# Down products of four feed-forward layers as seven block products

## The chip, the cores and the metric

One core of one Trainium2 chip runs the whole program in one launch. The metric is the device time of an execution in microseconds (us); lower is better. The median of the runs before is 3422.52 us.

## The reference, cut to what matters

Three network blocks are applied one after the other to x, 512 tokens of 1024 features, all in float32. Four feed-forward layers are in them; each has a wide first product, a nonlinearity, and a product back to 1024 features, the *down product*:

```
# layers 1 and 2 (first block): 2816 hidden features
x = layer_norm(ALPHA * x + 0.5 * ((silu(x @ w_gate) * (x @ w_up)) @ w_down))
# layer 3 (second block): 2816 hidden features, a short convolution over tokens on both halves
h = gelu(conv(u[..., :2816])) * conv(u[..., 2816:]);   x = x + rmsnorm(h @ w_down)
# layer 4 (third block): 4096 hidden features
x = x + gt2 * (square(relu(h @ w1)) @ w2)
```

Between the layers stand three mixers (attention, state-space and delta nets), which the change leaves as they are, but for where their temporaries lie.

## The kernel before, in words

Every float32 operand of the large products is held as two float32r tiles, high digits and low digits, so that a product is three matmuls: high x high, low x high, high x low. A matmul is 128 x 128 by 512 columns.

**Weights.** `slab` (L262 to L274) loads 1024 columns of weights into a `raw` tile (three buffers, DMA on the SP queue), makes the high digits `whi_t` by a cast on ACT (L268) and the low digits `wlo_t` by a subtraction on DVE (L272). `whi_t` and `wlo_t` have three buffers each, so the cast of a new slab waits until TensorE has read an old one for the last time. In some stages POOL takes a part of L272's columns.

**Feed-forward layers.** `ffn` (L630) cuts the hidden features into chunks of four tiles of 128 (the first chunk of layers 1 to 3 has two; these layers have six chunks, layer 4 has eight). Within a chunk, `hidden` runs `fm` (L338 to L340) for two tiles at a time: gate and then up weights in layers 1 to 3, the one matrix in layer 4. A call of `fm` is two slabs of 24 matmuls. The result is taken out of PSUM by ACT and DVE (L698 and L702 in layers 1 and 2, L1188 and L1191 in layer 3, L1527 and L1528 in layer 4) and split into digits (`split`, L257 on ACT and L258 on POOL or DVE). The down product of a chunk, `tm` (L379 to L381), follows the next chunk's first two hidden tiles (the first four in layer 4): four slabs, each used for all four tiles of 128 tokens, 24 matmuls a slab, 96 in all. Its sums are added on DVE to an SBUF tile (L709 in layers 1 and 2, L1214 in layer 3, L1537 in layer 4), eight times 128x512 a chunk. The last chunk goes through `tail` (L452 to L454).

**What sets the order.** Each engine runs its instructions in a fixed order, made when the program is built; a slab's cast and subtraction stand some places ahead of the matmuls that need them. In layer 2, `fill` also puts between the hidden tiles the third block's `modulation` (L1249 to L1262): 48 loads of 512 KB, each multiplied and added on DVE (L1249, L1251), and six times a split and two short products whose sums DVE adds to a row (L1262).

```
due = hh, hl, f1 - f0, f0          # a chunk's hidden features, for `tm` one step later
for c in range(2):
    self.linear_tm(down, due[2], range(c * 512, c * 512 + 512), due[:2], ..., k0=due[3])
```

Of the kernel before, what the change touches and what calls it, by code (L numbers as in the profile page):

```python
# [8 lines left out]
F32 = mybir.dt.float32  # L9
# [6 lines left out]
P = 128  # L16
# [6 lines left out]
SPACE = 25 * 1024 - 320  # L23
# [10 lines left out]
def constants():  # L34
    """What depends on shapes alone: masks and distances, each [P, n]."""
# [36 lines left out]
class Space:  # L72
    """Columns of a tile that parts of the computation take and give back."""

    def __init__(self, pool, n, dt, name):
        self.ap = pool.tile([P, n], dt, name=name)
        # when each granule was given back last, or None while it is taken
        self.free, self.clock = [0] * (n // GRAIN), 0

    def take(self, n):  # L80
        """The offset of n columns: those that have been free for longest."""
        g = -(-n // GRAIN)
        free, best, run = self.free, None, 0
        for i, f in enumerate(free):
            run = run + 1 if f is not None else 0
            if run >= g:
                edge = (i < g or free[i - g] is None) + (i + 1 == len(free) or free[i + 1] is None)
                key = (max(free[i - g + 1:i + 1]), -edge, i)
                if edge and (best is None or key < best):
                    best = key  # L90
        if best is None:
            raise MemoryError("no room for %d columns in %d" % (n, GRAIN * sum(f is not None for f in free)))
        a = best[2] - g + 1
        free[a:a + g] = [None] * g
        return a * GRAIN

    def give(self, a, n):
        self.clock += 1
        g = -(-n // GRAIN)
        self.free[a // GRAIN:a // GRAIN + g] = [self.clock] * g  # L100


class Room:
    """Tiles for a part of the computation, which leave() gives back; a tag names a ring of `bufs` of them."""

    def __init__(self, net, bufs=1):
        self.net, self.bufs, self.rings = net, bufs, {}

    def tile(self, shape, dt=F32, tag=None, name=None, bufs=None):
# [3 lines left out]
        if tag not in self.rings:  # L113
            self.rings[tag] = [0, n, space, [space.take(n) for _ in range(bufs or self.bufs)]]
# [4 lines left out]
        t = space.ap[:shape[0], a:a + n]  # L119
# [12 lines left out]
class Rows:  # L132
    """Tiles of four tiles of features each, read as one."""

    def __init__(self, tiles):
        self.tiles = tiles

    def __getitem__(self, at):
        return self.tiles[at[1] // 4][(at[0], at[1] % 4) + at[2:]]


class Net:
    def __init__(self, ctx, tc, shapes):
# [9 lines left out]
        self.spaces = {F32: Space(sp, SPACE, F32, "space"), F32R: Space(sp, SPACE_R, F32R, "space_r")}  # L153
        self.xt = pool("xt", 1)
        self.vec = Room(self, 3)
# [9 lines left out]
    def masks(self):  # L165
        """What all parts use; the first products come before."""
# [9 lines left out]
    def lay(self, shape, recipe):  # L176
        """An input of the program: `recipe` lays it out from the kernel's own."""
# [22 lines left out]
    def columns(self, pool, name, parts):  # L200
        """Vectors of features with features on partitions, a column for each 128: [P, sum of rows]."""
# [3 lines left out]
    def rowvec(self, name, n=D, off=0, pool=None, tag="vec"):  # L205
        """A vector of features on every partition."""
# [1933 lines left out]
```

## Time and profile before

| | |
|---|---|
| runs (us) | 3422.52, 3427.88, 3419.94; median 3422.52 |
| profiled execution, first to last instruction | 3421.3 us span |
| TensorE busy | 3302.2 us, 97% |
| VectorE (DVE) busy | 1910.4 us, 56% |
| ScalarE (ACT) busy | 1302.5 us, 38% |
| GpSimd (POOL) busy | 704.7 us, 21% |
| weight loads | 530 of 512 KB, 3.3 us from issue to landing (median) |

The profiled execution's own time is known by its span, which is 1.2 us under the median of the runs. A busy TensorE is one whose matmuls follow each other; their modelled ends overlap, so the distance of two starts tells the rate. Columns of a group of instructions: line, engine, operation, output and inputs, shapes, count, busy us, mean ns of one, idle time before them and who ended it.

### The profile page before, as it was taken

How to read it: one execution, taken by the hardware profiler on the slowest of the kernel's cores; microseconds unless marked ns; L12 is line 12 of the kernel's file. 1: busy time of each engine (PE TensorE's matmuls, PEld its weight loads, DVE VectorE, ACT ScalarE, POOL GpSimd, SP SyncE). 2: the span in 40 equal slices, each digit the busy share in tenths (PEclk: the TensorE clock that was granted, in tenths of full speed). 3: DMA queues.
4: the chain of work that ended last, by engine and by line, in shares of the span. 5: the costliest groups of instructions: out<-in, count | busy, mean ns of one | idle time of the engine just before them, and what ended most of it. 6: DMA issues, size and time to landing. Idle time of an engine off the chain costs nothing. (4 is left out here: it accounts for less than half of the span.)

```text
span 3421.3 us, 41640 instructions
## 1 busy us (share of the span) xinstructions
PE 3302.2 (97%) x16104; PEld 2687.0 (79%) x16104; DVE 1910.4 (56%) x2922; ACT 1302.5 (38%) x2158; POOL 704.7 (21%) x569
## 2 busy tenths in 40 slices
PE   9999999999999999988999999998999999999998
PEld 8888877777787888876777888887876777788886
DVE  4333657567648565565544465556676475463445
ACT  4222367233333322244342353333366222244333
POOL 0110301334323111132102240003210224130003
PEclk9999999999999999999999999999999999999999
DMA  5222321221225454331132332222411212232222
GB/s 196 95 99 98 136 70 56 77 77 65 83 87 195 155 174 166 130 137 65 64 105 87 111 113 99 99 93 99 137 56 50 71 53 78 93 118 105 99 97 88
DMA packets 105254, 348.59 MB, mean 102 GB/s; under 512 B 13836, under 2 KB 19020, under 8 KB 104800
## 3 DMA queue, kind: packets, MB, share of 16 engines
q1 hardware_dynamic: 105056, 345.93, 29.4%
q8 instruction: 127, 2.08, 0.2%
q14 instruction: 71, 0.58, 0.1%
HBM read 337.46 MB, written 8.42 MB: 101 GB/s over the span
## 5 line engine op out<-in xcount | busy, mean ns | idle before, releaser
L272 DVE TENSOR_TENSOR wlo_t<-raw,whi_t 128x1024 fp32r<-128x1024 f32 (+3 forms) x538 | 674.4, 1255 | 742.5 <-ACT whi_t L268 721.3
L268 ACT CAST whi_t<-raw 128x1024 fp32r<-128x1024 f32 (+1 forms) x538 | 560.6, 1043 | 1160.9 <-PE acc L339 614.7
L338 PE MATMUL acc<-xhi,whi_t 128*128 128x512 f32 x2160 | 856.9, 397 | 0.0
L339 PE MATMUL acc<-xlo,whi_t 128*128 128x512 f32 x2160 | 849.9, 393 | 0.0
L340 PE MATMUL acc<-xhi,wlo_t 128*128 128x512 f32 x2160 | 847.8, 393 | 0.0
L338 PEld LDWEIGHTS acc<-xhi,whi_t 128*128 128x128 f32 x2160 | 406.9, 188 | 88.2 <-issue 9.5
L339 PEld LDWEIGHTS acc<-xlo,whi_t 128*128 128x128 f32 x2160 | 407.2, 189 | 82.6 <-issue 4.8
L340 PEld LDWEIGHTS acc<-xhi,wlo_t 128*128 128x128 f32 x2160 | 406.9, 188 | 83.1 <-issue 0.7
L379 PE MATMUL acc<-whi_t,space_r 128*128 128x512 f32 x752 | 293.3, 390 | 1.2 <-DVE space L709 1.2
L380 PE MATMUL acc<-whi_t,space_r 128*128 128x512 f32 x752 | 293.1, 390 | 1.0 <-DVE space_r L258 1.0
L381 PE MATMUL acc<-wlo_t,space_r 128*128 128x512 f32 x752 | 292.3, 390 | 0.0
L258 POOL TENSOR_TENSOR space_r<-space,space_r 128x512 fp32r<-128x512 f32 x44 | 81.2, 1848 | 524.7 <-ACT space_r L257 524.7
L379 PEld LDWEIGHTS acc<-whi_t,space_r 128*128 128x128 f32 x752 | 141.2, 188 | 31.7 <-ACT whi_t L268 1.6
L380 PEld LDWEIGHTS acc<-whi_t,space_r 128*128 128x128 f32 x752 | 141.2, 188 | 30.9 <-DVE space_r L258 1.9
L381 PEld LDWEIGHTS acc<-wlo_t,space_r 128*128 128x128 f32 x752 | 141.2, 188 | 29.3
L338 PE MATMUL acc<-space_r,whi_t 128*128 128x512 f32 x384 | 152.0, 400 | 0.4 <-ACT space_r L257 0.4
L339 PE MATMUL acc<-space_r,whi_t 128*128 128x512 f32 x384 | 150.9, 393 | 0.0
L340 PE MATMUL acc<-space_r,wlo_t 128*128 128x512 f32 x384 | 150.7, 393 | 0.0
L379 PE MATMUL acc<-whi_t,xhi 128*128 128x512 f32 (+1 forms) x384 | 149.8, 390 | 0.4 <-ACT space L247 0.4
L257 ACT CAST space_r<-space 128x512 fp32r<-128x512 f32 x139 | 85.7, 618 | 158.9 <-DVE space L702 60.7
L381 PE MATMUL acc<-wlo_t,xhi 128*128 128x512 f32 (+1 forms) x384 | 143.7, 374 | 0.0
L380 PE MATMUL acc<-whi_t,xlo 128*128 128x512 f32 (+1 forms) x384 | 143.7, 374 | 0.0
(448 smaller groups left out, 5193.1 us busy)
## 6 DMA issues: line engine op xcount, KB each, us to landing
raw<-in SPq DMA_DIRECT2D x530, 512.0 KB, 3.3
space<-in SPq DMA_DIRECT2D x69, 512.0 KB, 4.4
space<-in SPq DMA_DIRECT2D x25, 256.0 KB, 3.7
x_keep<-space SPq DMA_DIRECT2D x12, 512.0 KB, 3.5
space<-x_keep SPq DMA_DIRECT2D x12, 512.0 KB, 4.4
space<-mod SPq DMA_DIRECT2D x6, 512.0 KB
space<-in SPq DMA_DIRECT2D x2, 1024.0 KB
raw<-in SPq DMA_DIRECT2D x8, 256.0 KB, 2.6
```

The lines of the kernel that those rows point to most:

```text
L257: self.nc.scalar.copy(dhi, src)
L258: (eng or self.nc.vector).tensor_sub(dlo, src, dhi.bitcast(F32))
L268: nc.scalar.copy(hi[:, :n], raw[:, :n])
L272: eng.tensor_sub(lo[:, c], raw[:, c], hi[:, c].bitcast(F32))
L338: nc.tensor.matmul(ps[j], whi[:, k, f], xhi[:, kk], start=kk == 0, stop=False)
L339: nc.tensor.matmul(ps[j], whi[:, k, f], xlo[:, kk], start=False, stop=False)
L340: nc.tensor.matmul(ps[j], wlo[:, k, f], xhi[:, kk], start=False, stop=kk == K - 1)
L379: nc.tensor.matmul(ps, xhi[:, kk, t], whi[:, k], start=kk == 0, stop=False)
L380: nc.tensor.matmul(ps, xlo[:, kk, t], whi[:, k], start=False, stop=False)
L381: nc.tensor.matmul(ps, xhi[:, kk, t], wlo[:, k], start=False, stop=kk == K - 1)
```

## The change

The down product of every chunk but a layer's last is done by seven block products in place of eight. Tokens, hidden features and output columns are halved each: a block is 256 tokens by half of the chunk's hidden tiles by 512 output columns. Seven sums and differences of hidden blocks (the *sides*) and seven of weight blocks are multiplied, and the products accumulate in two pairs of PSUM tiles, from which DVE adds or subtracts the running sums into the result.

- `sides` makes for each pair of hidden tiles, from four blocks of 256 tokens in a tile `t8`, four further blocks (L666 on POOL, L667 and L668 on DVE) and the digits of seven (three casts L670 on ACT, three subtractions L671 on POOL, of 256, 1024 and 512 columns).
- `seven` loads the four weight blocks into tiles `wd` of their own (L684) and adds them up in place (L695, on DVE; in layer 3 on POOL), four times a chunk; each of seven steps splits its block (L275 on ACT, L276 on DVE; buffers of `whi_t` and `wlo_t` as before), does 12 matmuls (L706) into the PSUM pairs `sc`, `sc` or `tr`, `o`, and hands both to `done` (L837, or L1276 in layers 3 and 4).
- `paced` puts the steps one by one between the 12-matmul pieces of the next chunk's `fm`.
- `modulation` takes its PSUM from `acc` in place of `sc`; 3584 columns of SBUF change hands between float32 temporaries and float32r operands (`lend`); the residual of layers 1 and 2 is scaled in place; small temporaries are placed by another rule. The digits of the last chunk's hidden features are made on POOL in all layers.

```diff
+    A12, A22, Z5, S3, S2, S4, A11, A21 = range(8)
+    def sides(self, t8, hi, lo, eng):
+        nc = self.nc
+        both = slice(self.Z5, self.S3 + 1)
+        eng.tensor_sub(t8[:, both], t8[:, self.A22:self.A11 + 1:5], t8[:, self.A21][:, None, :].to_broadcast([P, 2, 256]))
+        nc.vector.scalar_tensor_tensor(t8[:, self.S2], t8[:, self.S3], -1.0, t8[:, self.A22], op0=ALU.mult, op1=ALU.subtract)
+        nc.vector.scalar_tensor_tensor(t8[:, self.S4], t8[:, self.S2], -1.0, t8[:, self.A12], op0=ALU.mult, op1=ALU.subtract)
+        for g in (slice(self.A11, self.A11 + 1), slice(self.Z5, self.A11), slice(0, self.Z5)):
+            nc.scalar.copy(hi[:, g], t8[:, g])
+            eng.tensor_sub(lo[:, g], t8[:, g], hi[:, g].bitcast(F32))
+    def seven(self, wp, w, k0, sides, done, eng):
...
+        for i in (0, 1, 3, 2):
+            raw[i] = wp.tile([P, WS], F32, tag="wd", name="wd", bufs=4)[:, :n * 512]
+            nc.sync.dma_start(raw[i], src[i])
+        b11, b12, b21, b22 = (raw[i] for i in range(4))
+        steps = ((self.A11, b11, None, 0, True, (0, 0), 1), (self.Z5, b11, b12, 1, True, (1, 1), -1),
+                 (self.S2, b11, b22, 0, False, (0, 1), -1), (self.S4, b22, None, 1, False, (0, 1), -1),
+                 (self.S3, b12, b22, 0, False, (1, 1), -1), (self.A12, b21, None, 1, True, (0, 0), 1),
+                 (self.A22, b11, b21, 0, False, (1, 0), 1))
...
+        for slot, b, more, bank, start, c, sign in steps:
+            if more is not None:
+                eng.tensor_add(b, b, more)
...
+            self.split(hi[:, :n * 512], lo[:, :n * 512], b)
...
+            if start:
+                ps[bank] = [self.psum(x) for x in (("sc", "sc"), ("tr", "o"))[bank]]
+            for r in range(2):
+                t = slice(r * P, r * P + P)
+                for k, (ah, al) in enumerate(sides):
+                    for i, (x, y) in enumerate(((ah, whi), (al, whi), (ah, wlo))):
+                        nc.tensor.matmul(ps[bank][r], x[:, slot, t], y[:, k], start=start and k + i == 0,
+                                         stop=k == n - 1 and i == 2, skip_group_check=not start)
+                tt = 2 * c[0] + r
+                done(tt, c[1], (tt, c[1]) not in seen, sign, ps[bank][r])
+                seen.add((tt, c[1]))
+            yield
...
             for w, K, cols, ev in reversed(parts):
-                self.linear_fm(w, K, cols, X, ev)
+                for _ in self.fm(w, K, cols, X, ev):
+                    self.due_next()
...
-                    if due:
-                        for c in range(2):
-                            self.linear_tm(down, due[2], range(c * 512, c * 512 + 512), due[:2],
-                                           lambda tt, ps, c=c: done(tt, c, due[3] == 0, ps), k0=due[3])
-                        due = None
-                due = hh, hl, f1 - f0, f0
+                while self.due:
+                    self.due_next()
+                if not plain:
+                    at, both = f0, [sides[i] for i in range((f1 - f0) // 2)]
+                    self.due = self.paced(self.seven(tp, down, at, both, lambda tt, c, f, sign, ps, at=at: done(tt, c, f and at == 0, sign, ps),
+                                                     eng or nc.vector), lead, 14 if step == 2 else 7, prep)
...
+    def paced(self, parts, lead, n, prep):
+        for _ in range(lead):
+            yield
...
+        for i in range(1, n - lead + 1):
+            while done * (n - lead) < 7 * i:
+                next(parts)
+                done += 1
+            yield
...
-            self.ffn(X, DFF // P, 2, hidden, "ffn_w_down_2", done, part, end)
+            self.ffn(X, DFF // P, 2, hidden, "ffn_w_down_2", done, part, end, eng=nc.gpsimd)
...
-                    ps = self.psum("sc")
+                    ps = self.psum()
```

The order of the instructions moves with it. DVE in layer 1, one chunk's turn before: the slabs' low digits (L272), the sums out of PSUM (L709) in fours, and the hidden tiles (L702):

```order
L272 TENSOR_TENSOR wlo_t_647<-raw_645,whi_t_646 128x1024
L709 SCALAR_TENSOR_TENSOR space_70<-acc_575,space_70 128x512
L709 SCALAR_TENSOR_TENSOR space_70<-acc_576,space_70 128x512
L709 SCALAR_TENSOR_TENSOR space_70<-acc_577,space_70 128x512
L709 SCALAR_TENSOR_TENSOR space_70<-acc_578,space_70 128x512
L272 TENSOR_TENSOR wlo_t_681<-raw_679,whi_t_680 128x1024
L272 TENSOR_TENSOR wlo_t_711<-raw_709,whi_t_710 128x1024
```

The same place now (L290 is `slab`'s subtraction, L276 that of a step, L695 the adding of weight blocks, L837 the sums out of PSUM, L830 a hidden tile):

```order
L276 TENSOR_TENSOR wlo_t_1289<-space_70,whi_t_1288 128x1024
L695 TENSOR_TENSOR space_70<-space_70 128x1024 x2
L276 TENSOR_TENSOR wlo_t_1322<-space_70,whi_t_1321 128x1024
L695 TENSOR_TENSOR space_70<-space_70 128x1024
L837 SCALAR_TENSOR_TENSOR space_70<-sc_1292,space_70 128x512
L837 SCALAR_TENSOR_TENSOR space_70<-sc_1293,space_70 128x512
L290 TENSOR_TENSOR wlo_t_1343<-raw_1341,whi_t_1342 128x1024
L276 TENSOR_TENSOR wlo_t_1362<-space_70,whi_t_1361 128x1024
L837 SCALAR_TENSOR_TENSOR space_70<-tr_1325,space_70 128x512
L695 TENSOR_TENSOR space_70<-space_70 128x1024
```

The sums out of PSUM come in twos, and between them stand the weight blocks' sums and the low digits of steps and slabs.

ACT in layer 4, between the first and the third step of a chunk, now (L1662 and L1664 are the relu and the square of a hidden tile, L670 the sides' high digits, L275 a step's cast, 23771 the second step and 23792 the third, 23822 the fourth):

```order
L670 CAST flex_22379<-space_70 128x256
L275 CAST whi_t_23771<-space_70 128x1024
L1662 ACTIVATE space_70<-acc_23652 128x512
L1664 ACTIVATE space_70<-space_70 128x512
L670 CAST flex_22379<-space_70 128x512
L670 CAST flex_22379<-space_70 128x1024
L275 CAST whi_t_23792<-space_70 128x1024
L275 CAST whi_t_23822<-space_70 128x1024
```

The cast of the third step's weights stands behind the sides of the chunk's first two hidden tiles, whose 1024 columns wait for L666 on POOL and L667 and L668 on DVE; before, nothing on ACT or DVE between two slabs waited for POOL in this layer.

DVE in layer 2, where a piece of the modulation falls beside the fourth step (L1385 is the multiply-add of a 512 KB load, L1396 the row's sum; 9730 the low digits of the fourth step):

```order
L290 TENSOR_TENSOR wlo_t_9713<-raw_9711,whi_t_9712 128x1024
L1385 SCALAR_TENSOR_TENSOR space_70<-space_70 128x1024
L830 TENSOR_TENSOR space_70<-acc_9549,space_70 128x512
L1396 TENSOR_TENSOR space_70<-space_70,acc_9700 1x512
L667 SCALAR_TENSOR_TENSOR space_70<-space_70 128x256
L1396 TENSOR_TENSOR space_70<-space_70,acc_9704 1x512
L668 SCALAR_TENSOR_TENSOR space_70<-space_70 128x256
L276 TENSOR_TENSOR wlo_t_9730<-space_70,whi_t_9729 128x1024
```

Here the step's low digits moved behind a load, a hidden tile, two short sums and the two sides of the newest pair.

## Rows read from the trace of the kernel before

**Rows 1.** The page: busy us (share of the span) and instructions of PE.
```profile
PE 3302.2 (97%) x16104; PEld 2687.0 (79%) x16104; DVE 1910.4 (56%) x2922; ACT 1302.5 (38%) x2158; POOL 704.7 (21%) x569
```
**Rows 2.** Busy time by stretch, layers 1 to 4: PE, PEld, DVE, ACT, POOL, clock, DMA.
```profile
85.00:281.00 196.00, 196.00 (x866) 162.40 (x866) 68.45 (x72) 51.60 (x61) 18.44 (x12) 1.00 0.28 97
1129.20:1325.00 195.80, 194.61 (x859) 160.87 (x858) 104.86 (x104) 54.09 (x63) 28.87 (x14) 1.00 0.48 161
2075.00:2271.00 196.00, 196.00 (x865) 161.82 (x864) 102.48 (x120) 69.10 (x84) 15.52 (x12) 1.00 0.28 97
3060.00:3357.00 297.00, 296.02 (x1385) 248.43 (x1384) 122.39 (x139) 116.15 (x155) 3.58 (x3) 1.00 0.29 101
```
**Rows 3.** Timeline of layer 1: start us, us, engine, line; a slab made.
```profile
298.34 0.39 PE L339 MATMUL acc<-xlo,whi_t 128*128 128x512 f32 x1
298.56 0.39 PE L340 MATMUL acc<-xhi,wlo_t 128*128 128x512 f32 x1
...
298.76 1.05 ACT L268 CAST whi_t<-raw 128x1024 fp32r<-128x1024 f32 x1 [3.85 <-PE acc L339]
...
299.85 1.23 DVE L272 TENSOR_TENSOR wlo_t<-raw,whi_t 128x1024 fp32r<-128x1024 f32 x1 [4.17 <-ACT whi_t L268]
```
**Rows 4.** Groups of DVE in 85:281 (layer 1, three chunks).
```profile
L272 DVE TENSOR_TENSOR wlo_t<-raw,whi_t 128x1024 fp32r<-128x1024 f32 x36 | 44.1, 1226 | 102.8 <-ACT whi_t L268 102.0
L709 DVE SCALAR_TENSOR_TENSOR space<-acc,space 128x512 f32<-128x512 f32 x24 | 16.5, 690 | 8.1 <-PE acc L381 8.0
L702 DVE TENSOR_TENSOR space<-acc,space 128x512 f32<-128x512 f32 x12 | 8.3, 692 | 16.4 <-POOL space_r L258 12.2 <-PE acc L340 4.2
```
**Rows 5.** Groups of DVE in 1129.2:1325 (layer 2): the modulation.
```profile
L1251 DVE SCALAR_TENSOR_TENSOR space<-space 128x1024 f32<-128x1024 f32 x21 | 31.0, 1475 | 14.2 <-DMA space<-in 14.0
L1262 DVE TENSOR_TENSOR space<-space,sc 1x512 f32<-1x512 f32 x6 | 3.8, 667 | 0.0
```
**Rows 6.** Layer 3, 2075:2271: groups of DVE and of POOL.
```profile
L1191 DVE SCALAR_TENSOR_TENSOR space<-acc,space 128x510 f32<-128x510 f32 x24 | 18.0, 749 | 0.9
...
L1204 POOL TENSOR_TENSOR space<-space 128x512 f32<-128x512 f32 x12 | 15.5, 1293 | 169.2 <-DVE space L1191 169.2
```
**Rows 7.** Layer 4, 3060:3357: groups of DVE and ACT.
```profile
L1537 DVE TENSOR_TENSOR space<-space,acc 128x512 f32<-128x512 f32 x40 | 27.5, 686 | 13.8 <-PE acc L381 13.4
...
L1528 ACT ACTIVATE space<-space 128x512 f32<-128x512 f32 x30 | 19.0, 633 | 0.9
...
L1527 ACT ACTIVATE space<-acc 128x512 f32<-128x512 f32 x30 | 17.8, 594 | 25.3 <-PE acc L340 24.6 <-PE acc L416 0.8
```
**Rows 8.** Timeline: POOL beside a single DVE subtraction (layer 1).
```profile
281.44 1.29 POOL L258 TENSOR_TENSOR space_r<-space,space_r 128x512 fp32r<-128x512 f32 x1 [39.01 <-ACT space_r L257]
...
283.57 1.23 DVE L272 TENSOR_TENSOR wlo_t<-raw,whi_t 128x1024 fp32r<-128x1024 f32 x1
...
284.17 1.78 POOL L258 TENSOR_TENSOR space_r<-space,space_r 128x512 fp32r<-128x512 f32 x1 [1.43 <-ACT space_r L257]
```
**Rows 9.** Timeline of layer 2: POOL beside a dense DVE.
```profile
1179.53 1.62 POOL L258 TENSOR_TENSOR space_r<-space,space_r 128x512 fp32r<-128x512 f32 x1 [28.60 <-ACT space_r L257]
1183.57 5.07 POOL L258 TENSOR_TENSOR space_r<-space,space_r 128x512 fp32r<-128x512 f32 x1 [2.42 <-ACT space_r L257]
...
1178.71 1.28 DVE L1251 SCALAR_TENSOR_TENSOR space<-space 128x1024 f32<-128x1024 f32 x1
1180.35 1.88 DVE L1251 SCALAR_TENSOR_TENSOR space<-space 128x1024 f32<-128x1024 f32 x1 [0.37 <-DMA space<-in]
...
1183.95 2.34 DVE L272 TENSOR_TENSOR wlo_t<-raw,whi_t 128x1024 fp32r<-128x1024 f32 x2
1186.22 3.50 DVE L1251 SCALAR_TENSOR_TENSOR space<-space 128x1024 f32<-128x1024 f32 x2
```
**Rows 10.** POOL over 1024 columns of float32, the one time it occurs (line L1349).
```profile
L1349 POOL TENSOR_TENSOR space<-space,c_tri_le x1: 2402/2402/2402, 1504.3 to 1504.3; 128x1024 f32<-128x1024 f32 x1
```

More of the change, by code (lines that the diff above doesn't have):

```diff
@@ L72 @@
 class Space:
[L75 to L80, printed above, removed]
-        g = -(-n // GRAIN)
[L83 to L90, printed above, removed]
-        if best is None:
[L92 to L95, printed above, removed]
@@ L97, in give, with __init__, add, drop @@
-    def give(self, a, n):
+    def __init__(self, ap):
+        self.parts, self.clock = [(ap, [0] * (ap.shape[1] // GRAIN))], 0
+    def add(self, ap):
+        self.parts.append((ap, [0] * (ap.shape[1] // GRAIN)))
+    def drop(self):
+        _, free = self.parts.pop()
+        assert None not in free
+    def take(self, n, first=False):
+        g = -(-n // GRAIN)
+        best = None
+        for p, (_, free) in enumerate(self.parts[:1] if first else self.parts):
+            run = 0
+            for i, f in enumerate(free):
+                run = run + 1 if f is not None else 0
+                if run >= g:
+                    edge = (i < g or free[i - g] is None) + (i + 1 == len(free) or free[i + 1] is None)
+                    key = (-p, -i if n <= 256 else 0, max(free[i - g + 1:i + 1]), -edge, i)
+                    if edge and (best is None or key < best):
+                        best = key
+        if best is None:
+            raise MemoryError("no room for %d columns in %s" % (n, [GRAIN * sum(f is not None for f in free) for _, free in self.parts]))
+        p, a = -best[0], best[4] - g + 1
+        self.parts[p][1][a:a + g] = [None] * g
+        return p, a * GRAIN
@@ L113, in tile @@
         if tag not in self.rings:
-            self.rings[tag] = [0, n, space, [space.take(n) for _ in range(bufs or self.bufs)]]
+            self.rings[tag] = [0, n, space, [space.take(n, self.first) for _ in range(bufs or self.bufs)]]
         ring = self.rings[tag]
@@ L518, in to_xT, with lend @@
             self.split(dh, dl, pt)
+    def lend(self, dt):
+        if self.flexed == dt:
+            return
+        if self.flexed:
+            self.spaces[self.flexed].drop()
+        self.flexed = dt
+        self.spaces[dt].add(self.flex.tile([P, FLEX], dt, tag="flex", name="flex"))
     def new_xT(self):
@@ L627, in normed_to_xT @@
         self.xfree(t)
-    def ffn(self, X, nff, step, hidden, down, done, part, end, feed=None, prep=None, close=None):
+    A12, A22, Z5, S3, S2, S4, A11, A21 = range(8)
[8 more added lines that the diff above has]
+            eng.tensor_sub(lo[:, g], t8[:, g], hi[:, g].bitcast(F32))
@@ L634, in ffn @@
+    def ffn(self, X, nff, step, hidden, down, done, part, end, feed=None, prep=None, close=None, eng=None):
+        nc = self.nc
         chunk = 4
@@ L637, in last @@
         def last(tt, c, ps):
-            (close or done)(tt, c, False, ps)
+            (close or done)(tt, c, False, 1, ps)
             part(tt, c)
@@ L661, in ffn @@
+                t8 = {}
                 for f in range(f0, f1, step):
[L662 removed]
+                    hidden(gp, f, step, lambda i, at=f - f0: dst(at + i), whole if f else first)
                     if f:
                         self.fill(5)
[L665 to L672 removed]
@@ L677, in ffn, with due_next @@
                 self.share = TS
-            self.tail(down, due[2], (0, 1), due[:2], last, k0=due[3])
+            X = [Rows([sides[j][i] for j in range(len(sides))], 2) for i in range(2)]
+            self.tail(down, f1 - f0, (0, 1), X, last, k0=f0)
+    def paced(self, parts, lead, n, prep):
+        for _ in range(lead):
+            yield
+        if prep:
+            prep()
+        done = 0
+        for i in range(1, n - lead + 1):
[3 more added lines that the diff above has]
+            yield
+        for _ in parts:
+            pass
+    def due_next(self):
+        if self.due and next(self.due, 1):
+            self.due = None
     def swiglu_norm(self, X, wg, wu, wd, lg, lb, then, feed=None, rows=None):
         nc = self.nc
-        y, stats, vecs = [], {}, []
+        stats, vecs = {}, []
         def prep():
```

139 lines of the change are left out of this document (89 added, 50 removed).

## The prediction

> **What bounds the kernel now.** I read the page's busy times first: TensorE is busy 97% of the span [rows 1], so the question is whether it is also without gaps in the stages that the change touches. The table by stretch answers: in layers 1, 3 and 4 it idles under 1 us in 196, 196 and 297 us, in layer 2 it idles 1.2, all at a clock of 1.00 of 2.4 GHz [rows 2]. There time is matmuls and nothing else: 866 in 196 us is 0.2263 us each, the distance of starts in the timeline [rows 3]. So a matmul less is worth 0.226 us, as long as everything that TensorE needs is there.
>
> What hides behind it: in the timeline a slab's cast starts when TensorE has read the old slab (298.76, released by L339), takes 1.05, and the subtraction ends at 301.08: 2.35 us from the end of the last reading matmul to the low digits [rows 3]. Before, the next two slabs of 24 matmuls (10.9 us) cover this.
>
> **What is removed.** A chunk of four tiles had 96 down matmuls and has 84, the half chunks 48 and 42. Layers 1 to 3 have one half and four whole chunks ahead of the tail: 54 fewer each; layer 4 seven: 84. In all 246 x 0.2263 = 55.7 us. The lists of the built programs agree (15,279 matmuls, now 15,033), so that the change doesn't do what it says is no case to weigh.
>
> **What is added, by engine, for a whole chunk.** I write u for 12 matmuls, 2.72 us. Layers 1 and 2: 23 u, 62.5 us.
> - DVE, layer 1: 15 low-digit subtractions of 1024 columns in place of 12, at 1.226 [rows 4], 18.4; 14 sums out of PSUM in place of 8, at 0.690 [rows 4], 9.7; 4 hidden tiles 2.8; 4 sums of weight blocks, not in the trace, at the same 1.226 (also two float32 inputs from SBUF; POOL's 2.40 [rows 10] is the upper end), 4.9; 4 sides of 256 columns at about 0.4, half of 0.75 for 510 [rows 6]. Together 37.4 of 62.5; before it was 23.0 of 65.2.
> - Layer 2 adds the modulation, in three chunks 31.0 + 3.8 of DVE and 14.0 of waiting for loads [rows 5]: 37.4 + 11.6 + 4.7 = 54 of 62.5.
> - Layer 3: 16 convolution taps at 0.75 [rows 6] in place of the hidden tiles' products, no sums of weights: 42 of 62.5. POOL: four products at 1.29 [rows 6], sides (2 x 2304 columns at 1.29 for 512: 11.6), four sums of 1024 columns at 2.40 [rows 10] to 2.58 (twice 1.29): 27.
> - Layer 4: 15 u, 40.7 us: 11 subtractions, 14 sums at 0.686 [rows 7], 4 weight sums, sides: 29.6 of 40.7, and 11.6 on POOL.
>
> ACT gains 3 casts of 1.05 and the sides (some 4 us); it stays under 60%. The loads stay 512 KB each, as many as before; on SP's queue the `wd` loads stand a chunk ahead of use, and only raw loads queue behind them, which run three slabs ahead. No average passes 90%, so the cost is in places, where a step's weights come late.
>
> **Where weights come late.** The three buffers now serve steps of 12 matmuls. From the order, a buffer is free 2 or 3 u ahead of need in layers 1 to 3 (5.4 or 8.2 us, against 2.35), but only 1 u ahead (2.72) for the third step in layer 4.
>
> *POOL and DVE.* A lone POOL subtraction took 1.29; one that began 0.60 before a DVE subtraction had ended took 1.78 [rows 8]. Beside a dense DVE one took 5.07, and DVE's pair of adds in the same time 3.50 where one alone takes 1.28; a DVE add that began under a running POOL subtraction took 1.88 [rows 9]. I take it that such pairs go one after the other. In the Trainium skill, "SBUF — State Buffer", section "Who interferes with whom", a DVE instruction with two SBUF inputs and a POOL instruction that reads SBUF exclude each other for the whole instruction. By that alone each meeting costs the later one up to all of the other's length, some 6 us more in layer 4 than I take; the rows agree with the waiting, and 1.88 shows that a part is the usual price.
>
> *Layer 4.* From the chunk's start: the second hidden tile's matmuls end at 4 u = 10.9. Ahead of its relu on ACT stands the second step's cast (1.05), then relu 0.59 and square 0.63 [rows 7]: 13.0. POOL's difference, 1.29, ends between 14.3 and 15.6, as it goes before or after a weight sum; two sides on DVE 0.8: 16.5; the cast of 1024 columns 1.05; the third step's cast 1.05: 18.7; its subtraction 1.23: 19.9. Wanted at 7 u + 0.45 = 19.5. POOL's own subtractions of 512 and 1024 columns (1.3 and 2.6) want to run just then; if DVE meets both, 22.6. So late by 0.4 to 3.1; I take 2.2, nearest to the order in which DVE goes first and meets the long one only: 7 x 2.2 = 15 of the 19 us that layer 4 saves.
>
> *Layer 2.* The fourth step's digits stand behind a hidden tile, two row sums and the two sides, which wait for POOL: from the end of the up matmuls 0.69 + 1.29 + 0.8 + 2 x 0.63 + 1.23 = 5.3, wanted at 2.72 + 0.9 (the modulation's four matmuls) + 0.45 = 4.1. Late by 1.2, more by a meeting with POOL or a load (14.0 over 21 adds is 0.7 each [rows 5]); six rows of modulation at 1.7: 10. Bounds: 3, if DVE's work ahead is done early; 25, if each of ten batches costs 2.5.
>
> *Layers 1 and 3.* The second gate slab of a pair, whose cast stands behind the sides too: from the end of the up matmuls a hidden tile 0.69, POOL's difference and low digits 2 x 1.29, a step's subtraction 1.23, two sides 0.8, two casts 2.1, its own subtraction 1.23: 8.6, and 11.2 if it meets a POOL subtraction of 1024 columns; wanted at 4 u + 0.45 = 11.3. So just in time at worst by this; I take 0.5 for each of eight chunks, 4, since POOL can meet DVE twice; bounds 0 and 12. In layer 3 the adds on POOL end some 3 us ahead of need, so I cost them at nothing; without that slack each late step would cost its lateness.
>
> The rest (residual in place, other columns for temporaries, the modulation's PSUM) I cost at nothing: 8 PSUM banks and the mixers' order of matmuls are as before, save some rearranged products in one mixer; a few us either way.
>
> **Sum.** 55.7 - 15 - 10 - 4 = 26.7; 3421.3 - 26.7 = 3394.6 for the execution profiled, which stands 1.2 under the median: **3396** for the median.
>
> **Rivals.**
> - *The cover holds.* If DVE's order leaves the slack that the averages promise, 5 to 20 us come back: 3370 to 3387. For it: DVE sat idle 102.8 us of 196 in layer 1 ahead of subtractions whose casts waited for TensorE [rows 3, 4], and a stall moves all later deadlines too. Against: the layer 4 sum above.
> - *All is given back.* Stalls of 42 to 62 us: layer 2 at its 25, layer 4 at its 3.1 (22), layers 1 and 3 at 12: 59, 3.3 more than is saved, 3426. The condition is that DVE meets POOL nearly each time.
> - *Slower: DVE held by POOL twice a chunk.* If POOL's two subtractions of 1024 columns each take the port just as a step's or slab's digits stand first on DVE, 2 x 2.58 in each of 19 whole chunks is 98 us against 55.7: 3465. It decides from 2.9 us a chunk on. Against it: in layers 1 to 3 a meeting of 2.6 still fits in 5.4 - 2.35 = 3.1 when nothing else stands ahead.
>
> **How the numbers follow.** The forecast's own span, 20 to 42 us given back, is 3387 to 3409, with 0.42; the cover holds 0.27; all given back, 3409 to 3429, 0.19; slower than that 0.12. No change means within 0.2%, 6.8 us, about what a measurement of this kernel can tell: faster 0.42 + 0.27 + 0.06 of the third case = 0.75, the same 0.13, slower 0.12. The range 3370 to 3427 leaves out some 0.03 below and 0.14 above.
>
> **What would show it.** In the profile after: 246 fewer PE instructions (15,858); whole chunks of 276 matmuls in 62.5 us in layers 1 and 3; in layer 4 TensorE waiting some 2 us a chunk, ahead of the third step, for DVE's low digits (L276), with POOL's L671 of 1024 columns beside it; in layer 2 waits ahead of the fourth step. Wrong it is, if layer 4's chunks take under 41.5 us or over 44, if the waits stand at other steps, or if mixers change by more than 5 us.

## The result, and the profile after

The changed kernel took 3443.97 us (median of 3439.24, 3443.97 and 3449.19) against 3422.03 before, both on one chip: a ratio of 1.0061, 95% interval 1.0045 to 1.0077 (ratios here are estimates over all the executions, not quotients of two medians). A fourth execution, of 8258.93 us, is left out, and so is one of 8407.40 of the kernel before, run beside experiments 9 and 10. The changed kernel is slower by 0.6%, some 21 us, where 26 us less were forecast. The execution profiled took 3439.24 us, with a span of 3437.5.

The page of the kernel after, busy us (share of the span) and instructions; to be read against [rows 1]:

```profile
PE 3271.8 (95%) x15858; PEld 2649.1 (77%) x15858; DVE 2239.7 (65%) x3222; ACT 1394.0 (41%) x2269; POOL 967.0 (28%) x725
```

TensorE has the 246 instructions less and is busy 30 us less, in a span that is 16 us longer: the matmuls were saved, and more than that went into waits. The same four stretches as in [rows 2], each counted from its layer's first matmul, in the kernel after (columns: stretch, length; busy us and count of PE, PEld, DVE, ACT, POOL; clock; DMA):

```profile
85.00:281.00 196.00, 196.00 (x866) 162.28 (x866) 128.10 (x128) 69.09 (x80) 45.86 (x27) 1.00 0.32 100
1117.40:1313.20 195.80, 190.28 (x835) 155.77 (x834) 156.56 (x161) 68.30 (x82) 48.53 (x26) 1.00 0.51 164
2058.80:2254.80 196.00, 192.16 (x844) 157.81 (x844) 149.24 (x153) 86.29 (x106) 85.75 (x51) 1.00 0.32 100
3041.70:3338.70 297.00, 271.91 (x1192) 222.18 (x1191) 203.82 (x201) 129.94 (x168) 84.98 (x55) 0.93 0.29 92
```

Layer 1 is still without a gap in this stretch. Layers 2 and 3 idle 5.5 and 3.8 us. Layer 4 idles 25 us of 297, and its clock is 0.93 where it was 1.00: 1192 matmuls where 1385 ran. By stage, from the first matmul of one to that of the next in the timelines of both kernels (us):

| stage | before | after | difference | matmuls saved x 0.2263 |
|---|---|---|---|---|
| layer 1 | 368.7 | 356.0 | -12.7 | -12.2 |
| mixer 1 | 725.3 | 726.1 | +0.8 | |
| layer 2 | 379.5 | 376.1 | -3.4 | -12.2 |
| mixer 2 | 532.5 | 531.6 | -0.9 | |
| layer 3 | 384.7 | 379.7 | -5.0 | -12.2 |
| mixer 3 | 657.5 | 660.5 | +3.0 | |
| layer 4, up to its closing products (`tail`) | 332.5 | 357.2 | +24.7 | -19.0 |
| layer 4, closing products | 24.9 | 35.6 | +10.7 | |
| ahead and behind | 15.7 | 14.8 | -0.9 | |

So layer 4 alone turns a gain into a loss. Six of its seven chunks' down products run late: the first loses 9.7 us, and the next five come 47.6 us apart, where 180 matmuls at full rate are 40.7; the seventh, beside which no sides are made, has no wait. The third step of one of the five, timeline of TensorE (start us, us, then the idle time before it and what ended it):

```profile
3226.85 0.39 PE L706 MATMUL o<-wlo_t,flex 128*128 128x512 f32 x1
3229.03 0.50 PE L706 MATMUL sc<-whi_t,flex 128*128 128x512 f32 x1 [1.78 <-ACT whi_t L275]
3229.36 0.40 PE L706 MATMUL sc<-whi_t,space_r 128*128 128x512 f32 x1
3231.61 0.80 PE L706 MATMUL sc<-wlo_t,flex 128*128 128x512 f32 x1 [1.85 <-DVE wlo_t L276]
3232.20 0.63 PE L706 MATMUL sc<-whi_t,flex 128*128 128x512 f32 x1
3232.63 0.63 PE L706 MATMUL sc<-whi_t,space_r 128*128 128x512 f32 x1
```

Two waits, each 2.0 us longer than the usual distance, and after them matmuls 0.43 us apart in place of 0.23. The table by stretch shows the latter as the granted clock, which falls to 0.50, that is 1.2 GHz, for some 7 us:

```profile
3228.00:3230.00 2.00, 0.73 (x2) 0.30 (x2) 1.08 (x2) 1.93 (x3) 1.90 (x1) 1.00 0.00 0
3230.00:3232.00 2.00, 0.39 (x1) 0.39 (x2) 2.00 (x2) 0.00 (x0) 0.47 (x1) 0.62 0.00 0
3232.00:3234.00 2.00, 2.00 (x6) 1.52 (x6) 2.00 (x4) 0.00 (x0) 0.00 (x0) 0.50 0.00 0
...
3236.00:3238.00 2.00, 2.00 (x7) 1.55 (x6) 1.72 (x2) 0.90 (x1) 0.00 (x0) 0.67 0.65 195
3238.00:3240.00 2.00, 2.00 (x10) 1.67 (x9) 0.16 (x1) 0.65 (x1) 0.00 (x0) 1.00 0.60 168
```

The 13 matmuls from 3231.61 on take 5.7 us in place of 2.9, which is 2.8 more; with the waits, 4.0, that is 6.8 of the 6.9 us by which a chunk is too long. What the third step waited for is read off the other engines' timelines:

```profile
3215.83 2.59 DVE L276 TENSOR_TENSOR wlo_t<-space,whi_t 128x1024 fp32r<-128x1024 f32 x1 [2.12 <-ACT whi_t L275]
3218.45 2.91 DVE L695 TENSOR_TENSOR space<-space 128x1024 f32<-128x1024 f32 x2
...
3222.53 1.22 DVE L695 TENSOR_TENSOR space<-space 128x1024 f32<-128x1024 f32 x1
3224.93 1.50 DVE L667 SCALAR_TENSOR_TENSOR space<-space 128x256 f32<-128x256 f32 x1 [1.18 <-POOL space L666]
3226.47 0.43 DVE L668 SCALAR_TENSOR_TENSOR space<-space 128x256 f32<-128x256 f32 x1
...
3229.01 2.55 DVE L276 TENSOR_TENSOR wlo_t<-space,whi_t 128x1024 fp32r<-128x1024 f32 x1 [0.92 <-ACT whi_t L275]
...
3214.93 2.41 POOL L671 TENSOR_TENSOR space_r<-space,flex 128x1024 fp32r<-128x1024 f32 x1 [1.96 <-ACT flex L670]
...
3222.60 2.30 POOL L666 TENSOR_TENSOR space<-space 128x512 f32<-128x512 f32 x1 [3.59 <-ACT space L1664]
3224.86 1.29 POOL L671 TENSOR_TENSOR space_r<-space,space_r 128x512 fp32r<-128x512 f32 x1
3228.10 2.37 POOL L671 TENSOR_TENSOR space_r<-space,space_r 128x1024 fp32r<-128x1024 f32 x1 [1.95 <-ACT space_r L670]
...
3220.18 1.05 ACT L275 CAST whi_t<-space 128x1024 fp32r<-128x1024 f32 x1 [2.08 <-DVE space L695]
...
3226.98 1.05 ACT L670 CAST space_r<-space 128x1024 fp32r<-128x1024 f32 x1 [3.87 <-DVE space L668]
3227.93 1.99 ACT L275 CAST whi_t<-space 128x1024 fp32r<-128x1024 f32 x2
```

The chain starts at the first step: its digits L276 take 2.59 beside POOL's L671 of 1024 columns, the weight sums L695 follow late, and so does the second step's cast on ACT (3220.18), which stands ahead of the second hidden tile. From this tile on, POOL's L666 takes 2.30 beside DVE's L695; L667, which needs it, takes 1.50 beside POOL's L671 of 512 columns, where the like L668, alone, takes 0.43; ACT's casts follow at 3226.98 and 3227.93; and the digits L276 of the third step take 2.55 beside POOL's next L671. Four meetings of DVE and POOL in these lines stand on the chain. It is the rule and not one case; groups of DVE and POOL in layer 4 (3062.8 to 3392):

```profile
L276 DVE TENSOR_TENSOR wlo_t<-space,whi_t 128x1024 fp32r<-128x1024 f32 x49 | 78.8, 1607 | 25.1 <-ACT whi_t L275 25.1
...
L667 DVE SCALAR_TENSOR_TENSOR space<-space 128x256 f32<-128x256 f32 x13 | 19.4, 1496 | 20.1 <-POOL space L666 20.1
...
L666 POOL TENSOR_TENSOR space<-space 128x512 f32<-128x512 f32 x13 | 22.8, 1756 | 68.5 <-ACT space L1664 68.5
```

The closing products of layer 4 wait for something else, POOL's queue (timeline of TensorE and POOL):

```profile
3401.11 0.79 PE L471 MATMUL acc<-whi_t,space_r 128*128 128x512 f32 x1 [6.02 <-POOL space_r L276]
...
3407.21 0.80 PE L471 MATMUL acc<-whi_t,space_r 128*128 128x512 f32 x1 [4.46 <-POOL space_r L276]
...
3398.57 1.26 POOL L1679 TENSOR_TENSOR space<-space 128x512 f32<-128x512 f32 x1
3399.79 1.26 POOL L276 TENSOR_TENSOR space_r<-space,flex 128x512 fp32r<-128x512 f32 x1
3401.01 2.49 POOL L1678 TENSOR_TENSOR space<-space 128x512 f32<-128x512 f32 x2
3403.46 2.48 POOL L1679 TENSOR_TENSOR space<-space 128x512 f32<-128x512 f32 x2
3405.89 1.26 POOL L276 TENSOR_TENSOR space_r<-space,flex 128x512 fp32r<-128x512 f32 x1
```

The low digits of the last hidden tiles (L276), which were DVE's in this layer, stand among the 16 operations of the close (L1678, L1679).

### The profile page after: what moved, and what is told of

The parts are those of the page before. It is cut to its first block, busy times and chain, and to the rows that moved or that the text cites. A ratio compares the mean times of both kernels' runs of the same rounds, so it can differ in the third digit from the quotient of the medians.

```text
span 3437.5 us, 41835 instructions
## 1 busy us (share of the span) xinstructions
PE 3271.8 (95%) x15858; PEld 2649.1 (77%) x15858; DVE 2239.7 (65%) x3222; ACT 1394.0 (41%) x2269; POOL 967.0 (28%) x725
## 5 line engine op out<-in xcount | busy, mean ns | idle before, releaser
L290 DVE TENSOR_TENSOR wlo_t<-raw,whi_t 128x1024 fp32r<-128x1024 f32 (+3 forms) x456 | 597.7, 1313 | 376.1 <-ACT whi_t L286 359.3
L286 ACT CAST whi_t<-raw 128x1024 fp32r<-128x1024 f32 (+1 forms) x456 | 475.1, 1043 | 776.7 <-PE acc L357 401.1
L276 DVE TENSOR_TENSOR wlo_t<-space,whi_t 128x1024 fp32r<-128x1024 f32 (+1 forms) x154 | 221.2, 1438 | 88.7 <-ACT whi_t L275 80.2
L275 ACT CAST whi_t<-space 128x1024 fp32r<-128x1024 f32 (+1 forms) x154 | 152.1, 992 | 198.6 <-PE acc L357 56.8
L671 POOL TENSOR_TENSOR space_r<-space,flex 128x256 fp32r<-128x256 f32 (+2 forms) x84 | 132.7, 1581 | 323.6 <-ACT flex L670 323.6
L706 PE MATMUL sc<-whi_t,space_r 128*128 128x512 f32 x432 | 157.2, 404 | 3.6 <-ACT whi_t L275 3.6
L290 POOL TENSOR_TENSOR wlo_t<-raw,whi_t 128x384 fp32r<-128x384 f32 (+1 forms) x72 | 92.7, 1289 | 210.5 <-ACT whi_t L286 205.8
L486 POOL TENSOR_TENSOR rstd<-ve,mhalf 128x1 f32<-128x1 f32 (+1 forms) x68 | 58.0, 854 | 291.0 <-DVE ve L484 255.3
L1188 POOL TENSOR_TENSOR space_r<-c_tri_le,space_r 128x512 fp32r<-128x512 f32 x64 | 86.6, 1378 | 182.7 <-PE sc L1190 124.5
L434 PE MATMUL acc<-xhi,wlo_t 128*128 128x256 f32 x448 | 130.6, 296 | 6.9 <-DVE wlo_t L290 5.8
```

What stands on the lines that cost most here:

```text
L275: self.nc.scalar.copy(dhi, src)
L276: (eng or self.nc.vector).tensor_sub(dlo, src, dhi.bitcast(F32))
L286: nc.scalar.copy(hi[:, :n], raw[:, :n])
L290: eng.tensor_sub(lo[:, c], raw[:, c], hi[:, c].bitcast(F32))
L671: eng.tensor_sub(lo[:, g], t8[:, g], hi[:, g].bitcast(F32))
L706: nc.tensor.matmul(ps[bank][r], x[:, slot, t], y[:, k], start=start and k + i == 0, stop=k == n - 1 and i == 2, skip_group_check=not start)
```

## The experiments

My theory after the traces: layer 4 loses by the third step's waits, which come from DVE and POOL meeting, and by the clock that follows; its closing products by POOL's queue. The rivals: something that lies ahead of layer 4 or runs through it (where temporaries stand), DVE being full, or POOL being merely slow. Times are medians; every ratio is to the kernel before, run on the same chip beside it. Stages are timed in the one execution profiled of each run.

**1. Is it layer 4?** Layer 4 with eight block products, layers 1 to 3 with seven:

```diff
-        self.ffn(X, 32, 4, hidden, "mlp_w2_3", done, part, end, close=close)
+        self.ffn8(X, 32, 4, hidden, "mlp_w2_3", done, part, end, close)
```

`ffn8` is the `ffn` of the kernel before.

> Edit: layer 4 takes its down products in eight block products as before the change; layers 1 to 3 keep the seven. Theory (all of the loss is layer 4's): that layer comes back to 332 us up to its closing products and 25 us for them, layers 1 to 3 keep their 21 us of gain (12.7, 3.4 and 5.0) and the mixers lose 3, so the time falls by some 35 us against the changed kernel and stands 13 us (0.4%) under the kernel before. Rival (the change costs layer 4 by what lies ahead of it, such as where the temporaries stand): layer 4 stays over 340 us with eight products too, and the time stays above the kernel before.

Measured: 3403.77 us, ratio 0.9959 (0.9944 to 0.9973). Layer 4 takes 332.5 us and 26.2 for its closing products. The rival falls: nothing outside layer 4's own down products, and what is made for them, slows it, and the change without them is faster than before by 0.4%.

**2. The sides on one engine.**

```diff
-                            self.sides(e[0], hi, lo, nc.gpsimd)
+                            self.sides(e[0], hi, lo, nc.vector if close else nc.gpsimd)
```

> Edit: in layer 4 alone the sums and digits of the hidden sides (L666, L671) are made on VectorE in place of GpSimd. Theory (late third step): each chunk loses 4.0 us in two waits at its third step, since the difference of L667 takes 1.5 us beside a GpSimd operation, the 1024-column cast follows it, and the digits L276 take 2.55 us beside GpSimd's L671; then about 2.8 us at half clock. On one engine L667 takes 0.3 to 0.5 us, the waits fall to 1 us or less, the clock stays at 1.0, and layer 4 up to its closing products falls from 357 us to 313 to 325; the time falls by 32 to 44 us. Rival (VectorE full): VectorE gets some 5.8 us more a chunk; its other digits come late, waits stand at other steps, and layer 4 stays over 345 us.

Measured: 3394.82 us, ratio 0.9930 (0.9915 to 0.9945). Layer 4 up to its closing products takes 314.3 us. Two groups of DVE in that layer (3035 to 3380) in this run:

```profile
L276 DVE TENSOR_TENSOR wlo_t<-space,whi_t 128x1024 fp32r<-128x1024 f32 x49 | 61.2, 1251 | 11.5 <-ACT whi_t L275 10.8
...
L667 DVE SCALAR_TENSOR_TENSOR space<-space 128x256 f32<-128x256 f32 x14 | 5.9, 418 | 0.0
```

And a stretch of layer 4, as long as the one of [rows 2]:

```profile
3040.00:3337.00 297.00, 296.00 (x1382) 247.17 (x1382) 236.95 (x289) 151.33 (x193) 9.05 (x7) 1.00 0.31 105
```

As dense as before the change [rows 2], with DVE busy 0.80 of the time, and no wait at a step. L667 fell from 1.50 to 0.42 us, L276 from 1.61 to 1.25. Of the 19.0 us that layer 4's matmuls are worth, 18.2 arrive. One edit of an engine's name is worth 43 us in layer 4.

Not all of it is the meetings. With the edit the build also ordered TensorE's matmuls otherwise: in six third steps the first low digits are wanted by the seventh matmul, where in the change it was the third (3231.61 above). Such a step in this run, TensorE and then DVE:

```profile
3203.38 0.39 PE L706 MATMUL sc<-whi_t,flex 128*128 128x512 f32 x1
...
3204.51 0.39 PE L357 MATMUL acc<-xlo,whi_t 128*128 128x512 f32 x1
3204.74 0.48 PE L706 MATMUL sc<-wlo_t,flex 128*128 128x512 f32 x1
...
3203.45 1.22 DVE L276 TENSOR_TENSOR wlo_t<-space,whi_t 128x1024 fp32r<-128x1024 f32 x1
```

In the old order the digits would be wanted at 3203.83, and they are there at 3204.67. So the new order hides some 0.9 us a chunk, 5 of the 43 us; that is an estimate from these lines, and no run has the edit without the new order. Experiments 3 and 6 to 10 have an order like it.

**3. The meeting, or POOL's slowness?** POOL keeps L666; only the low digits L671 go to DVE, so that nothing of POOL stands beside L667 or the third step's L276:

```diff
-        eng.tensor_sub(t8[:, both], t8[:, self.A22:self.A11 + 1:5], t8[:, self.A21][:, None, :].to_broadcast([P, 2, 256]))
+        nc.gpsimd.tensor_sub(t8[:, both], t8[:, self.A22:self.A11 + 1:5], t8[:, self.A21][:, None, :].to_broadcast([P, 2, 256]))
```

on top of the edit of experiment 2.

> Edit: in layer 4 alone GpSimd keeps the 512-column difference of the sides (L666), and VectorE makes their low digits (L671), so that no GpSimd operation stands beside L667 or beside the third step's digits. Theory (two engines at one memory port, which go one after the other): L667 takes 0.4 us in place of 1.5 and the digits L276 of the third step 1.22 in place of 2.55; the second wait (2.02 us) goes, the first (1.95) falls to about 0.9, the clock stays at 1.0, and layer 4 up to its closing products takes 313 to 325 us, near the run with both on VectorE (314). Rival (GpSimd is only the slower engine, and L666 at 1.3 us in place of 0.7 is what makes the third step late): the first wait stays over 1.5 us and layer 4 takes 325 to 345 us.

Measured: 3403.63 us, ratio 0.9950 (0.9930 to 0.9970); layer 4 takes 321.7 us up to its closing products, its chunks come 41.9 us apart, and the clock stays at 1.00. One wait is left in a chunk (timeline of TensorE):

```profile
3210.15 0.50 PE L706 MATMUL sc<-wlo_t,flex 128*128 128x512 f32 x1 [0.61 <-DVE wlo_t L276]
```

L667 takes 0.42 and L276 1.22, as the theory says, and the layer lies in its range; but the wait left is the one for the digits, and not the one for the cast, as I had expected. Of the 42.9 us between the change and experiment 2, 35.5 go with L671's place, and 7.4 with L666's, which still took 2.38 us beside DVE in one such place. The 35.5 are the meetings, the clock that they cost, and the changed order of the third step, which shows here too (five matmuls stand ahead of the low digits).

**4. Time in place of speed.** The third step one piece of a product later:

```diff
-            while done * (n - lead) < 7 * i:
+            while (done + 1) * (n - lead) <= 7 * i if n == 7 else done * (n - lead) < 7 * i:
```

> Edit: in layer 4 alone the seven steps go in bursts of two, two and three in place of three, two and two, so that the third step stands behind one more piece of twelve matmuls (2.72 us). Theory (late third step): what its waits of 1.95 and 2.02 us are short of is time from the hidden tiles to the step; 2.72 us more leave 1.3 us of them or less, too little for the clock to fall, and layer 4 up to its closing products goes from 357 us to 315 to 330; the time falls by 27 to 42 us. Rival (port): the low digits of the third step take 2.55 us wherever they stand, since GpSimd's 1024-column digits move with them; a wait of about 2 us stays, the clock with it, and layer 4 takes 335 to 350 us.

Measured: 3414.10 us, ratio 0.9984 (0.9975 to 0.9993); layer 4 takes 331.7 us, where the theory said 315 to 330 and the rival 335 to 350. The 2.72 us took the wait for the cast away, and the low digits, still 2.59 us beside POOL, are late at two steps (timeline of TensorE):

```profile
3220.40 0.50 PE L706 MATMUL sc<-wlo_t,flex 128*128 128x512 f32 x1 [1.24 <-DVE wlo_t L276]
...
3223.87 0.50 PE L706 MATMUL tr<-wlo_t,flex 128*128 128x512 f32 x1 [0.45 <-DVE wlo_t L276]
```

Chunks come 43.1 us apart, 40.7 and 2.0 of waits, and the clock stays at 1.00 from the second chunk on. So half the wait costs a third of the loss, and with it the clock no longer falls. The layer's time lies between the two theories, and both hold a part: time mends the cast's wait, and the meeting moves along with the step.

**5. The closing products.**

```diff
-                            self.split(hi[:, i % 2], lo[:, i % 2], t, nc.gpsimd)
+                            self.split(hi[:, i % 2], lo[:, i % 2], t, nc.vector if close else nc.gpsimd)
```

> Edit: in layer 4 alone the digits of the last chunk's hidden tiles are made on VectorE in place of GpSimd. Theory (queue): layer 4's closing products wait 6.0 and 4.5 us because their digits stand on GpSimd behind the sixteen operations of the close, and TensorE then runs at half clock; with the digits on VectorE the closing products take 25 to 26 us as before the change (35.6 after it), the stage up to them stays at 357 us, and the time falls by 9 to 11 us. Rival (the close itself is late): the closing products wait for what the close makes, whoever makes the digits; they stay at 34 to 36 us and the time does not move.

Measured: 3432.98 us, ratio 1.0042 (1.0027 to 1.0057). The closing products take 27.3 us, 8.3 less; the stage before them 357.8. POOL's queue it was, if a little less than the 9 to 11 expected: waits of 1.5 us for the digits, now DVE's, and of 2.5 for a slab's cast are left.

**6. Both in layer 4** (the edits of 2 and 5):

> Edit: the two that helped together: in layer 4 the sides' operations and the last chunk's digits on VectorE. Theory (two causes apart from one another): layer 4 takes 314 us up to its closing products, as with the sides alone, and 25 to 28 us for these, so the time is 7 to 10 us under that run's 3395, 3385 to 3388, about 1% under the kernel before. Rival (VectorE, with 0.8 of its time taken, gives the gain of the one back): the closing products stay over 32 us, or the stage before them takes over 320, and the time is 3391 or more.

Measured: 3388.82 us, ratio 0.9905 (0.9890 to 0.9921). 314.4 us and 28.8 for the closing products: the two causes add up but for 1.5 us, and the time is a little over the range given.

**7. Layer 2's modulation, spread** (on top of 6):

```diff
                 for _ in self.fm(w, K, cols, X, ev):
                     self.due_next()
+                    self.fill(0.625)
...
-                    if f:
-                        self.fill(5)
```

> Edit: as the run before it, and in layer 2 the parts of the modulation follow each piece of a gate or up product one by one (0.625 of a part for each of 80 pieces) in place of five in a row after each pair of hidden tiles. Theory (bursts): the waits of layer 2 at steps' and slabs' digits (3.3, 1.9 and three of about 1 us) come from the five modulation rows that stand in a row on VectorE; spread, at most 3 us of the 8.3 are left, layer 2 up to its closing products falls from 345.5 to 339 to 342 us, and the time by 4 to 6 us against the run before it. Rival (VectorE full in layer 2, at 0.78 to 0.87 of its time): the waits only move to other steps, and layer 2 stays at 344 to 348 us.

Measured: 3387.19 us, ratio 0.9902 (0.9888 to 0.9917), no difference to 6 that these runs can tell. In the profile layer 2 takes 342.6 us up to its closing products, against 345.6: the fourth step's waits of 3.1 and 1.6 us became one of 1.1, with one of 0.5 at a third step, but those at slabs stayed, one of 1.9 us among them. The waits of the stage fell by 1.0 us in all, from 7.3 to 6.3; the granted clock, 0.50 for 3.4 us behind the fourth step's wait in run 6, stayed at 1.00 here, which is most of the rest. Bursts are a part of it at most.

**8. Layer 3 too** (on top of 6): the sides on DVE where `close or eng`.

> Edit: as the run of both edits in layer 4, and in layer 3 too the sides' operations on VectorE. Theory (the same late third step, smaller): layer 3 waits 0.8 to 1.2 us a chunk at the low digits of its third step and these go; up to its closing products it takes 338 to 339 us in place of 342, and the time falls by 3 to 4 us against the run of both. Rival (VectorE full): VectorE, 0.76 of its time taken in layer 3, goes to 0.85, digits of slabs come late, and layer 3 takes 342 us or more.

Measured: 3382.68 us, ratio 0.9887 (0.9870 to 0.9903). Layer 3 takes 336.7 us up to its closing products, against 342.1 in 6; the third steps' waits are gone, and two at slabs, of 0.6 and 1.1 us, are left. The stretch 2026 to 2337, run 6 and then this one:

```profile
2026.00:2337.00 311.00, 305.98 (x1342) 250.82 (x1340) 226.81 (x241) 135.35 (x170) 133.40 (x83) 1.00 0.29 96
```
```profile
2026.00:2337.00 311.00, 309.67 (x1381) 256.39 (x1380) 232.20 (x282) 140.72 (x177) 83.69 (x46) 1.00 0.30 100
```

POOL is busy 50 us less, and DVE, on which the same operations take 27 us (0.69 for L666, 1.22 for 1024 columns of L671), is busy only 5.4 us more: its own got shorter by some 22.

**9. 7 and 8 together:**

> Edit: the sides on VectorE in layers 3 and 4, layer 4's last digits on VectorE, and the modulation spread over the pieces of layer 2. Theory (three gains apart from one another): layer 2 up to its closing products 342 to 343 us, layer 3 337, layer 4 314, and the time 1 to 4 us under the run without the spread modulation (3382.7). Rival (the spread modulation gains nothing that can be measured): within 2 us of it.

Measured: 3382.96 us, ratio 0.9893 (0.9877 to 0.9908): layer 2 342.6, layer 3 336.4, layer 4 314.4, and no gain over 8 in the time. The rival holds for the time.

**10. The sides on DVE in all layers**, with the modulation in its bursts:

```diff
-                            self.sides(e[0], hi, lo, nc.vector if (close or eng) else nc.gpsimd)
+                            self.sides(e[0], hi, lo, nc.vector)
```

> Edit: the sides on VectorE in all four layers, the modulation in bursts of five as in the change. Theory (collision): GpSimd's operations beside VectorE's cost VectorE as much time as it would take to do them: in layer 3 some 50 us of work that left GpSimd raised VectorE's busy time by only 5.4 us (226.8 to 232.2 in 2026 to 2337). In layer 2 the nine pairs then cost 26 us and give back some 23 (L290 from 1365 to 1225 ns, L1385 from 1439 to 1270, L667 from 1434 to 420), so VectorE stays at about 0.80 of its time, layer 1 stays at 330 us and layer 2 up to its closing products takes 340 to 347. Rival (VectorE full): in layer 2, at 0.80 before, VectorE goes to 0.88 of its time, the steps' digits come late behind the modulation's rows, and layer 2 takes 350 us or more.

Measured: 3374.68 us, ratio 0.9871 (0.9854 to 0.9889): the fastest of all, 1.3% under the kernel before. Layer 1 takes 329.0 us up to its closing products and layer 2 336.3, below what either theory said: no wait is left ahead of layer 2's closing products. (In run 8 the clock was 0.50 for 6.8 us of layer 2, here not at all: some 3 of the 11 us by which the stage is shorter.) The stretch 1113 to 1430, run 8 and then this one:

```profile
1113.00:1430.00 317.00, 309.59 (x1346) 253.62 (x1345) 252.90 (x259) 110.25 (x129) 68.48 (x39) 0.99 0.47 155
```
```profile
1113.00:1430.00 317.00, 315.89 (x1390) 260.16 (x1389) 258.87 (x304) 114.01 (x132) 17.43 (x9) 1.00 0.48 160
```

DVE's group of slab digits in the same stretch, again run 8 and then this one:

```profile
L290 DVE TENSOR_TENSOR wlo_t<-raw,whi_t 128x1024 fp32r<-128x1024 f32 x38 | 50.8, 1340 | 6.7 <-ACT whi_t L286 6.5
```
```profile
L290 DVE TENSOR_TENSOR wlo_t<-raw,whi_t 128x1024 fp32r<-128x1024 f32 x38 | 45.9, 1216 | 1.2 <-ACT whi_t L286 1.2
```

DVE is 0.80 busy before and 0.82 after, in a stretch that holds 44 matmuls more. It was never full; it was held.

## Why the prediction was wrong

The sign was wrong, and the time lies above the range, which ended at 3427. Of the 43 us between the span forecast and the one measured, 28.7 are layer 4 up to its closing products and 10.7 these; the rest, 3.5 in all, is spread over the other stages.

- **What is saved: right.** 246 instructions less; where nothing waits, the matmuls arrive as time (layer 1 -12.7 against 12.2; layer 4 in experiment 2, 18.2 of 19.0).
- **Layers 1 and 3, 4 us given back: too much for 1, too little for 3.** Layer 1 gave nothing back, layer 3 7.2. Half of that is the third step's, 0.8 to 1.2 us a chunk, which I had looked for in layer 4 alone; two slabs wait 2.5 more. The adds of weights on POOL that I costed at nothing cost little: they are still there in experiment 8, with 1.7 us of waits left.
- **Layer 2, 10 us: right in size (8.8), in part by luck.** I took six rows of modulation to make the fourth step 1.7 us late each; two fourth steps were late, by 3.3 and 1.9 us, and three slabs by 0.9 to 1.1, which the sum does not hold. The chain had both the rows and POOL's difference in it, and POOL weighs more: experiment 7 spread the rows and gained 3 us of the stage at most, experiment 10 left them and took the sides off POOL, and all waits went.
- **Layer 4, 15 us: the step that failed.** Place and chain were as put (third step, low digits L276, POOL's L671 beside them), the size was 43.7 us: 24.7 lost where 19.0 were to be gained, 6.9 us in each of five chunks that I priced at 2.2, 9.7 in the first and nothing in the last. Of the 6.9, the late step is 4.0 and the clock 2.9. The chain of the chunk shown above, in us from its start (19.04, which is 7 u, ahead of 3227.08, where the third step would have begun):

  | end of | in the sum | measured |
  |---|---|---|
  | square of the second hidden tile | 13.0 | 14.4 |
  | POOL's difference | 14.3 to 15.6 | 16.9 |
  | two sides on DVE | 16.5 | 18.9 |
  | the third step's cast | 18.7 | 20.9 |
  | its low digits (wanted at 19.5) | 19.9, at most 22.6 | 23.5 |

  Two terms were mis-sized. The second step's cast, put ahead of the relu at its own 1.05, started 1.2 us late, because its weight sum had waited behind the first step's digits, which met POOL (2.59). "Two sides on DVE 0.8" took 1.9, since the first meets POOL's 512-column subtraction. POOL's difference, 2.30, was inside its bounds, and the last subtraction's 2.55 inside what I allowed for meetings; but the bound of 22.6 is itself a slip, for 19.9 with both meetings, 1.3 and 2.6, is 23.8. The third term was missing: the clock, which halved during the second wait and cost the other 2.9 us. I read the clock of 1.00 before [rows 2] as given, when waits can bring it down.
- **"The rest I cost at nothing": wrong by 10.7 us.** In layer 4 the change moves the last tiles' low digits from DVE to POOL, among the 16 operations of the close. The order showed it; I looked at products and not at that split. The mixers changed by 0.8, -0.9 and 3.0 us, within the 5 that I named; where the last comes from was not tried.
- **The rivals.** "Slower: DVE held by POOL twice a chunk" named the mechanism and the point from which it decides, 2.9 us a chunk. Layer 4 passed that with 6.9, and layers 1 to 3 did not. The two meetings of 1024 columns are there in layer 4 (2.59 and 2.55), at 1.3 us each in place of the 2.58 put in; the rest of the 6.9 is the shorter meetings ahead of them and the clock. I gave it 0.12, as if it had to hold in all layers at once; one layer sufficed.

On the Trainium skill: the rule of "SBUF — State Buffer", section "Who interferes with whom", is that a DVE instruction with two inputs in SBUF and a POOL instruction that reads SBUF exclude each other for the whole instruction. By the prediction's own account it would have added 6 us in layer 4. This case's rows side with the rule. In layer 4 of the changed kernel 33 operations of DVE (14 of L667, 13 of L276, 6 of L695) start while POOL's L671 runs, and each takes longer than alone by what is left of POOL's operation, less 0.13 to 0.15 us: L667 at 3224.93 by 1.08, with 1.22 left; L276 at 3229.01 by 1.33, with 1.46 left. The row of 1.88 us [rows 9], from which I took that a part is the usual price, says the same: POOL's subtraction (1179.53, 1.62) had 0.80 left, and the add took 0.60 more than its 1.28. A part was paid because a part was left.

## What to carry to other kernels

Where two engines hold each other up, as DVE and POOL do here, work moved from one to the other is not all taken off the first: count each meeting as a stop for the later one until the earlier has ended, on both sides, and try a short chain of dependent steps on one engine, even a busy one. When steps get shorter, cost each step's chain against its own deadline in every stage; a stage where the buffer's slack is least decides the sign. And when an operation changes engines, look at what stands ahead of it in the new queue at the end of the stage as well.

## What the hardware showed that I had not expected

TensorE's clock fell from 2.4 to 1.2 GHz during the second of two waits of 2.0 us with two matmuls between them, in five chunks of layer 4 (in the first chunk at the end of a wait of 4.0), and came back some 7 us later; in experiment 4 waits of 1.4 and 0.6 us left it at 1.00. So a wait's price is not its length: the 4.0 us cost 6.9 a chunk.

Nor is it the same each time. In layer 2 of the changed kernel a single wait of 3.3 us left the clock at 1.00; in experiments 1 to 6 and 8 the wait at the same matmul, 3.0 to 3.4 us, went with 0.50 for 3.4 us (in 8 for 6.8). The wait, then two us of the clock behind it in the changed kernel and in run 6:

```profile
1272.71 0.50 PE L706 MATMUL tr<-wlo_t,flex 128*128 128x512 f32 x1 [3.13 <-DVE wlo_t L276]
```
```profile
1272.00:1274.00 2.00, 1.29 (x6) 1.07 (x7) 2.00 (x3) 0.65 (x1) 1.27 (x1) 1.00 0.22 31
```
```profile
1272.00:1274.00 2.00, 2.00 (x7) 1.58 (x6) 2.00 (x2) 0.33 (x1) 1.59 (x1) 0.53 0.85 254
```

What decides between the two was not tried.

A 256-column operation on DVE took three and a half times as long beside POOL (1.50 against 0.42 us), and 50 us of POOL's busy time, moved to DVE, raised DVE's by 5.4 us (experiment 8).
